# Layer B's keys and values as one Strassen product with tokens on the partitions, and the plain chunk given to the first queries

## The chip, the cores and the metric

The kernel runs on one core of a Trainium2 chip. The metric is the device time of one launch in microseconds (us), the median of three runs. The core's engines are TensorE (PE, with its weight loads as PEld), VectorE (DVE), ScalarE (ACT), GpSimd (POOL) and SyncE (SP), which here issues the DMAs. They run side by side and wait for one another by semaphores. PE writes its sums to PSUM, eight banks of 128 partitions x 512 f32; only DVE and ACT carry them from there to SBUF.

## The reference

A decoder trunk of two layers on 512 tokens of width 2048. Layer A is a sparse attention; layer B, the one in question, is a stick-breaking attention with 16 query heads over 4 shared heads of keys and values, each 128 wide. Cut to what the change touches:

```python
x = layer_norm(ALPHA * x + mixer_a(x, ...), ...)
x = x + per_layer_embed(x, p[0], ...)          # stream after layer A: 512 x 2048
k, v = jnp.split(x @ w_kv, [512], axis=-1)     # shared keys, values: 512 x 512 each
q, gate = jnp.split(x @ w_in, [2048], axis=-1) # layer B's queries and gate
o = stick_breaking(q, k, v)
h = (o * silu(gate)) @ w_o
```

All matrices are f32. `w_kv` is 2048 x 1024, its first 512 columns for the keys, the others for the values.

## The kernel before

**Numbers and products.** The stream lies transposed in SBUF: a block of 128 features by 512 tokens for each of 16 blocks (`NK`). To keep f32 precision every operand is split into a high and a low part (`split`, L140 and L141: one ACT copy to fp32r makes the high part, one DVE subtraction the low one), and each product is three matmuls (`mm3`: high x high, high x low, low x high). `XH[k]`, `XL[k]` are the parts of the stream; `F[0]` to `F[3]` hold four f32 blocks each, and `fblock(n)` is the n-th of the 16.

**Weights.** `units` lists the weight blocks in the order in which they are used. `next_raw` keeps up to three of them on the way (the tile `raw`, three buffers of 512 KB, issued by SP in order). A stream of items takes them, splits them into `wh`, `wl` and, for Strassen, `sh`, `sl` (three buffers each) and hands them to the loop that issues the matmuls. `Ahead(items, 2)` makes two items ahead of the one in use. PE's order is the program's; DVE's and ACT's is set by a scheduler, except where `paced` or `pinned` keeps the program's order.

**The stage.** At the end of layer A the stream of layer B is finished block by block. Then:

- A plain chunk (`gemm_w`, banks 0 to 3, 192 matmuls of 512 columns): the keys, four blocks of 128 columns, weights as the fixed operand, tokens moving. While it runs, `first_chunk` still splits the last blocks of the stream (`build_plain`) and makes the sums of token halves that Strassen needs (`stream_sums` into `C3`; `turn_first` writes the difference t1 over the second half of `XH[k]`, `XL[k]`).
- Five Strassen chunks (`gemm_s`, in Winograd's form, seven products in seven banks): the values, then the queries of the four groups into `F[0]` to `F[3]`. Each handles 512 output columns: the inner dimension is halved (rows k and k+8 together), the tokens are halved (256 columns per matmul) and the output blocks too. A chunk is 16 items of 21 matmuls. For each unit DVE makes four sums of weight quarters (`prepare`, s1 to s4), and each item is split in two operations on ACT and two on DVE.
- After a chunk `combine` takes the seven products together into the four quarters of the result; what it need not do at once goes into the list `bg`, whose entries `pumped_at` puts between the matmuls of the next chunk.
- In the second Strassen chunk `turn_values` transposes the values (16 transposes on PE, one ACT copy for every four), because the attention wants tokens on the partitions for them. After the fourth, `split_values` and `split_keys` write the parts that the attention uses.

The line numbers in the profile are those of this kernel; the code of DVE and ACT that goes through the wrapper `Paced` has L116 or L118, the matmuls of `mm3` have L145 to L147.

Of the kernel before, what the change touches and what calls it, by code (L numbers as in the profile page):

```python
# [18 lines left out]
T = 512  # L19
H = T // 2  # L20
D = 2048
NK = D // 128
# [55 lines left out]
def trunk_kernel(  # L78
# [17 lines left out]
    pe = nc.tensor  # L96
    pinned = [False]
# [39 lines left out]
    def bank(i, name="ps"):  # L137
        return psum.tile([128, 512], F32, name=name, tag=f"bank{i}")

    def split(hi, lo, src, eng=dve):  # L140
        act.activation(hi, src, AF.Copy)  # L141
        eng.tensor_tensor(lo, src, hi.bitcast(F32), ALU.subtract)

    def mm3(out, a, b, start, stop):
        pe.matmul(out, a[0], b[0], start=start, stop=False)  # L145
        pe.matmul(out, a[0], b[1], start=False, stop=False)  # L146
        pe.matmul(out, a[1], b[0], start=False, stop=stop)  # L147

    ident = top.tile([128, 128], F32, name="ident")
# [35 lines left out]
    halves = []  # L185
    sent = [0]

    def next_raw():
        while sent[0] < len(units) and len(raws) < 3:
            raw = top.tile([128, 2, 512], F32, name="raw", tag="raw", bufs=3)  # L190
            unit = units[sent[0]]
            if len(unit) == 1:
                _, k, n = unit[0].shape
            else:
                k, n = 2, unit[-1]
            raw = raw.rearrange("p a n -> p (a n)")[:, : k * n].rearrange("p (k n) -> p k n", k=k)
            if len(unit) == 1:
                nc.sync.dma_start(raw, unit[0])
            else:
                src, a, b, c0, n = unit  # L200
# [12 lines left out]
            raws.append(raw)  # L213
            sent[0] += 1
        return raws.popleft()
# [38 lines left out]
    def weight_parts():  # L254
        return tuple(top.tile([128, 512], F32R, name=n, tag=n, bufs=3) for n in ("wh", "wl"))
# [94 lines left out]
    def paced(fn, *args):  # L350
        was, pinned[0] = pinned[0], True
        fn(*args)
        pinned[0] = was
# [61 lines left out]
    def strassen_stream(widths, wp):  # L415
        return Ahead(strassen_items(widths, wp), 2)

    def product_banks(first):
# [25 lines left out]

    def combine(wp, M, dst):

# [20 lines left out]

    def combine_last(wp, M, dst):

# [68 lines left out]
    PAIRS = [n for k in range(8) for n in (k, k + 8)]  # L538
# [93 lines left out]
    items = Ahead(all_items(), 2)  # L632
# [85 lines left out]
    ps = bank(4, "ik")  # L718
# [15 lines left out]
    banks = late_banks(range(4))  # L734
    gemm = gemm_w(items, late_plain, banks)
# [32 lines left out]
    banks = [bank(b, "v") for b in (4, 5, 6, 7)]  # L768
# [5 lines left out]
    K = [tuple(pkv.tile([128, T], F32R, name=f"k{s}{g}") for s in "hl") for g in range(4)]  # L774
    V = [tuple(pkv.tile([128, 512], F32R, name=f"v{s}{t}") for s in "hl") for t in range(4)]
# [52 lines left out]
    for g in range(4):  # L828
        banks = [bank(b + 4 * (g % 2), "q") for b in range(4)]
# [69 lines left out]
    for g in range(4):  # L899
        banks = mm_banks("g")  # L900
# [256 lines left out]
    TF, T1, C3 = [], [], []  # L1157
# [35 lines left out]
    V, K = ([tuple(spots[n : n + 2]) for n in where] for where in ((0, 2, 4, 6), (8, 14) * 2))  # L1193
    Q, A = ([tuple(spots[n : n + 2]) for n in where] for where in ((18, 12, 16, 10), (20, 22)))

    def split_keys(g):
        split(*K[g], Kf[:, g])

    def split_values(t):
        split(*(v.rearrange("p (g d) -> p g d", g=4) for v in V[t]), Vf[:, :, t * 128 : (t + 1) * 128])  # L1200

    def split_scaled(g, i):
        qh, ql = (q.rearrange("p (h q) -> p h q", h=4) for q in Q[i])
# [3 lines left out]

    with tc.tile_pool(name="sp", bufs=1) as sp:
        Kf, Vf = shared
        banks = [bank(b, "k") for b in range(4)]  # L1210
# [5 lines left out]
        def turn_values(t):  # L1216
            s = slice(t * 128, (t + 1) * 128)
            ps = bank(2, "vt")
            for g in range(4):
                pe.transpose(ps[:, g * 128 : (g + 1) * 128], Vf[:, g, s], ident)  # L1220
            act.activation(Vf[:, :, s], ps.rearrange("p (g d) -> p g d", g=4), AF.Copy)

        for n, dst in enumerate((Vf, *F)):
            M = product_banks(4 - n)
            gemm = pumped_at(gemm_s(items, C3, M), (13, 20, 27, 34, 41, 53, 65, 77, 89, 101, 104, 107, 110))
            if n == 1:
                steps(gemm, 40)
                for t in range(4):
                    steps(gemm, 16)
                    turn_values(t)  # L1230
            run(gemm)
            drain()
            if n == 4:
# [4 lines left out]
            if n == 3:  # L1238
# [31 lines left out]
    class Sticks:  # L1270
# [3 lines left out]
        units = [(3, 3), (1, 1), (3, 2), (1, 0), (3, 1), (2, 2), (3, 0), (2, 1), (0, 0), (2, 0)]  # L1274
# [163 lines left out]
    banks = mm_banks("g")  # L1438
    items = Fed(items)
    gemm = gate_first(banks)  # L1440
# [13 lines left out]
    for g in range(4):  # L1454
# [20 lines left out]
        if g < 3:  # L1475
# [4 lines left out]
            banks = mm_banks("g")  # L1480
            gemm = gemm_w(items, plain, banks)
# [59 lines left out]
```

## Time and profile before

| | us |
|---|---|
| time, median of 3 runs | 1863.06 (1862.87 to 1863.2) |
| the profiled execution, its own time | 1863.64 |
| its span, first to last instruction | 1861.9 |
| plain chunk (keys) | 987.5 to 1031.0 |
| five Strassen chunks | 1031.0 to 1234.3 |
| transposes of the values | 1091.4 to 1110.3 |

The page gives one execution. Its busy times say how much of the span an engine worked; the chain of waits says which work, followed back from the end, set the end. A view of stretches gives, for chosen windows, the busy time and number of instructions of each engine, the clock granted to PE, the DMA engines' share and their rate. The timeline lists single instructions with start, duration, engine, line and operation, and, in brackets, how long the engine had idled and for whom. Matmuls overlap: their duration is longer than the distance to the next start.

### The profile page before, as it was taken

The page shows a single profiled execution, that of the slowest core. Times are in us where ns is not written, and L with a number is a line of the kernel's source. Part 1 is how long each engine was busy: PE and PEld are TensorE (multiplying, and loading weights), DVE is VectorE, ACT ScalarE, POOL GpSimd, SP SyncE. Part 2 cuts the span into 40 slices and gives each one's busy share as a digit, 9 for nine tenths or more (in the row PEclk, how much of TensorE's full clock was granted, in tenths as well). Part 3 has the DMA queues.
Part 4 walks back from the last instruction along what each step waited for, and adds up shares of the span by engine and source line. Part 5 has one row for each costly group of instructions (what it writes and reads, how often), then busy time and mean ns, then how long its engine had stood idle before and what let it go on. Part 6 is the DMA issues. An engine that isn't in the chain of part 4 may idle for free.

```text
span 1861.9 us, 24820 instructions
## 1 busy us (share of the span) xinstructions
PE 1854.8 (100%) x9181; PEld 1576.4 (85%) x9181; DVE 1230.9 (66%) x2395; ACT 937.7 (50%) x1688; POOL 11.8 (1%) x28
## 2 busy tenths in 40 slices
PE   9999999999999999999999999999999999999998
PEld 8898888888888888888888999988888888888887
DVE  5668678566556444676468788888878745567534
ACT  3546333355555432375245444468888733347422
POOL 0000000000000000000000000001000000000000
PEclk9999999999999999999999999999999999999999
DMA  6442333322222432332434333322122252233333
GB/s 198 128 115 68 93 100 92 101 62 71 72 60 66 159 114 85 110 111 92 140 114 129 103 103 103 103 91 91 57 69 78 69 191 92 79 125 99 116 102 114
DMA packets 111178, 189.21 MB, mean 102 GB/s; under 512 B 8528, under 2 KB 29008, under 8 KB 111056
## 3 DMA queue, kind: packets, MB, share of 16 engines
q1 hardware_dynamic: 111056, 187.62, 33.0%
q8 instruction: 72, 1.18, 0.3%
q14 instruction: 50, 0.41, 0.1%
HBM read 179.21 MB, written 8.39 MB: 101 GB/s over the span
## 4 chain that ended last, share of the span: by engine, by line
PE 97%; DVE 2%; ACT 1%; issue 0%; DMA 0%; SPq 0%
PE g L145 12%; PE g L147 12%; PE g L146 12%; PE o L147 7%; PE o L145 7%; PE o L146 7%; PE m L145 4%; PE m L147 4%; PE m L146 4%; PE q L147 3%; PE q L145 3%; PE q L146 3%; PE k L146 2%; PE k L147 2%; PE k L145 2%; PE iq L147 1%
## 5 line engine op out<-in xcount | busy, mean ns | idle before, releaser
L118 ACT ACTIVATE wh<-raw 128x512 fp32r<-128x512 f32 (+2 forms) x624 | 359.5, 577 | 685.4 <-PE g L146 219.6
L118 DVE TENSOR_TENSOR wl<-raw,wh 128x512 fp32r<-128x512 f32 (+2 forms) x623 | 387.8, 623 | 437.1 <-ACT wh L118 421.7
L145 PE MATMUL g<-xh,wh 128*128 128x512 f32 x1024 | 403.5, 394 | 0.0
L147 PE MATMUL g<-xh,wl 128*128 128x512 f32 x1024 | 399.5, 390 | 0.0
L146 PE MATMUL g<-xl,wh 128*128 128x512 f32 x1024 | 399.3, 390 | 0.0
L147 PEld LDWEIGHTS g<-xh,wl 128*128 128x128 f32 x1024 | 192.2, 188 | 41.0
L146 PEld LDWEIGHTS g<-xl,wh 128*128 128x128 f32 x1024 | 192.5, 188 | 37.2
L145 PEld LDWEIGHTS g<-xh,wh 128*128 128x128 f32 x1024 | 192.4, 188 | 36.9
L147 PE MATMUL o<-xh,wl 128*128 128x512 f32 x512 | 199.3, 389 | 0.0
L146 PE MATMUL o<-xl,wh 128*128 128x512 f32 x512 | 199.2, 389 | 0.0
L145 PE MATMUL o<-xh,wh 128*128 128x512 f32 x512 | 199.2, 389 | 0.0
L147 PEld LDWEIGHTS o<-xh,wl 128*128 128x128 f32 x512 | 96.1, 188 | 20.4 <-DVE wl L118 0.5
L146 PEld LDWEIGHTS o<-xl,wh 128*128 128x128 f32 x512 | 96.1, 188 | 20.0
L145 PEld LDWEIGHTS o<-xh,wh 128*128 128x128 f32 x512 | 96.1, 188 | 19.9
L145 PE MATMUL q<-xh,wh 128*128 128x512 f32 x256 | 99.6, 389 | 0.0
L146 PE MATMUL q<-xl,wh 128*128 128x512 f32 x256 | 99.6, 389 | 0.0
L147 PE MATMUL q<-xh,wl 128*128 128x512 f32 x256 | 99.6, 389 | 0.0
L118 ACT ACTIVATE sh<-st 128x512 fp32r<-128x512 f32 x80 | 49.7, 624 | 44.5 <-DVE st L118 44.3
L116 ACT ACTIVATE wk<-z 128x512 f32<-128x512 f32 x80 | 47.9, 598 | 38.7 <-DVE z L116 15.2
L118 DVE TENSOR_TENSOR sl<-st,sh 128x512 fp32r<-128x512 f32 x80 | 55.2, 691 | 13.9 <-ACT sh L118 13.9
L118 DVE TENSOR_TENSOR xl<-f,xh 128x512 fp32r<-128x512 f32 x80 | 54.3, 686 | 12.6 <-ACT f L118 12.3
L146 PEld LDWEIGHTS q<-xl,wh 128*128 128x128 f32 x256 | 48.0, 188 | 10.1
(298 smaller groups left out, 3401.4 us busy)
## 6 DMA issues: line engine op xcount, KB each, us to landing
raw<-w_in_a SPq DMA_DIRECT2D x95, 512.0 KB, 3.7
raw<-w_in_b SPq DMA_DIRECT2D x64, 512.0 KB, 3.8
raw<-w_ple_gate SPq DMA_DIRECT2D x52, 512.0 KB, 3.7
raw<-w_o_a SPq DMA_DIRECT2D x24, 512.0 KB, 3.8
raw<-w_o_b SPq DMA_DIRECT2D x24, 512.0 KB, 3.7
raw<-w_kv_b SPq DMA_DIRECT2D x16, 512.0 KB, 3.8
raw<-w_ple_gate SPq DMA_DIRECT2D x24, 256.0 KB, 2.9
f<-xT SPq DMA_DIRECT2D x4, 1024.0 KB, 6.4
```

What stands on the lines that cost most here:

```text
L116: ins = method(*args, **kw)
L118: ins = method(*args, **kw)
L145: pe.matmul(out, a[0], b[0], start=start, stop=False)
L146: pe.matmul(out, a[0], b[1], start=False, stop=False)
L147: pe.matmul(out, a[1], b[0], start=False, stop=stop)
```

## The change

The plain chunk and the two operands change places. The plain chunk now makes the queries of the first group into `F[0]`. The keys and values become one Strassen product of 512 tokens by 1024 columns: the stream's parts are the fixed operand (128 tokens at a time), the weights move (512 columns per matmul), and the result has tokens on the partitions. Its quarters are tokens 0 to 255 and 256 to 511 by keys and values: c11, c12 are the halves of `Kf`, c21, c22 those of `Vf`. Seven products take two banks each, so they run in three passes of 4, 4 and 6 banks, with `kv_items` reading the weights again in each pass: 8 + 8 + 16 transfers of 512 KB where there were 16. As values now come out with tokens on the partitions and keys do not come out as wanted, `turn_keys` transposes the keys in place of `turn_values` (the same number of transposes), in the query chunk for `F[2]`, and three query chunks follow in place of the values' and four.

- First pass: items are the two halves of a raw block, split and used (m2, m4). Second: the first half, and the difference s3, made by DVE (m1, m7). Third: per k, two raw blocks; POOL makes s1, DVE s2 and s4, and each of the three is split (m6, m5, m3). An item is one pair of tiles of 512 columns and feeds six matmuls. Items are made four ahead (`Ahead(kv_items(sp), 4)`), and the splits use `sh`, `sl` and `wh`, `wl` in turn.
- Up to six raw blocks are on the way in this part: every second one goes into a free half of `F[2]` or `F[3]` (`homes`).
- After the first pass ACT copies m2 and m4 out; after the second ACT copies m1 and m7, DVE adds m1 onto c11, POOL adds c22 onto c21 (1024 columns); at the end of the third ACT copies m5 and m3, DVE adds m6 onto u and m5 onto c22, and POOL does the last four sums, 1024 columns each. They replace a `combine`.
- The first query chunk's items (two) are made after 42 of the third pass's 48 steps.

In the program as built POOL's order is four of the s1 sums, the add of c22 onto c21, the other four s1 sums, then the four adds at the end. In SP's order the first transfers into `F[2]` and `F[3]` stand between the eight weight blocks of the plain chunk.

```diff
-        while sent[0] < len(units) and len(raws) < 3:
-            raw = top.tile([128, 2, 512], F32, name="raw", tag="raw", bufs=3)
+        while sent[0] < len(units) and len(raws) < (6 if sent[0] in kv_units else 3):
+            raw = homes.get(sent[0])
+            if raw is None:
+                raw = top.tile([128, 2, 512], F32, name="raw", tag="raw", bufs=3)
...
+    def kv_items(wp):
+        made = [0]
+        temps = [F[1][:, n] for n in range(4)]
+        for _ in range(2):
+            st = wp.tile([128, 4 * H], F32, name="st", tag="st", bufs=2)
+            temps.extend(st[:, n * T : (n + 1) * T] for n in range(2))
...
+        for k in range(8):
+            raw = next_raw()
+            for a in range(2):
+                yield parts(a, raw[:, a])
+        for k in range(8):
+            raw = next_raw()
+            s3 = temp()
+            dve.tensor_tensor(s3, raw[:, 0], raw[:, 1], ALU.subtract)
+            yield parts(0, raw[:, 0])
+            yield parts(1, s3)
+
+        def sums():
+            r0 = next_raw()
+            r1 = next_raw()
+            s1, s2, s4 = temp(), temp(), temp()
+            pool.tensor_tensor(s1, r0[:, 1], r1[:, 1], ALU.add)
+            dve.tensor_tensor(s2, s1, r0[:, 0], ALU.subtract)
+            dve.tensor_tensor(s4, r1[:, 0], s2, ALU.subtract)
+            return s2, s1, s4
+
+        ready = sums()
+        for k in range(8):
+            three = ready
+            for n, src in enumerate(three):
+                if n == 2 and k < 7:
+                    ready = sums()
+                yield parts(3 * k + n, src)
+
+    def gemm_quarters(items, products):
+        for k in range(NK // 2):
+            for get, outs in products:
...
+                w = next(items)
...
+                h, l = get(k)
+                for j, out in enumerate(outs):
+                    s = slice(j * 128, (j + 1) * 128)
+                    mm3(out, (h[:, s], l[:, s]), w, k == 0, k == NK // 2 - 1)
+                    yield
...
-    add_job(w_kv_b, 0, strassen=True)
-    add_job(w_kv_b, 512, strassen=True)
-    for g in range(4):
+    add_job(w_in_b, 0, strassen=True)
+    kv_rows = w_kv_b.rearrange("(k p) (a n) -> k p a n", p=128, a=2)
+    for k in (*range(8, NK), *range(8), *PAIRS):
+        kv_units.add(len(units))
+        if len(kv_units) % 2 == 0:
+            homes[len(units)] = (F[2][:, 0:2], F[2][:, 2:4], F[3][:, 0:2])[len(kv_units) // 2 % 3]
+        units.append((kv_rows[k],))
+    for g in range(1, 4):
         add_job(w_in_b, g * 512, strassen=True)
...
-        items = first_chunk(gemm, TF, T1, C3, lambda: strassen_stream([512] * 5, sp))
-        for g in range(4):
-            act.activation(Kf[:, g], banks[g], AF.Copy)
+        items = first_chunk(gemm, TF, T1, C3, lambda: Ahead(kv_items(sp), 4))
+        for h in range(4):
+            act.activation(F[0][:, h], banks[h], AF.Copy)
...
+        m2, m4 = pair(4, "m2"), pair(6, "m4")
+        run(gemm_quarters(items, ((half(8, 0), m2), (summed(2), m4))))
...
+        m1, m7 = pair(0, "m1"), pair(2, "m7")
+        run(gemm_quarters(items, ((half(0, 0), m1), (summed(1), m7))))
+        for j in range(2):
+            paced(act.activation, u[:, j], m1[j], AF.Copy)
+            paced(dve.tensor_tensor, c11[:, j], c11[:, j], m1[j], ALU.add)
+        for j in range(2):
+            paced(act.activation, c22[:, j], m7[j], AF.Copy)
+        pool.tensor_tensor(c21, c21, c22, ALU.add)
+
+        m6, m5, m3 = pair(4, "m6"), pair(6, "m5"), pair(0, "m3")
+        gemm = gemm_quarters(items, ((summed(0), m6), (half(0, H), m5), (half(8, H), m3)))
+        steps(gemm, 42)
+        pinned[0] = True
+        items = strassen_stream([512] * 3, sp).prime()
+        pinned[0] = False
...
+        pool.tensor_tensor(c21, c21, u, ALU.add)
+        pool.tensor_tensor(c22, c22, u, ALU.add)
+        pool.tensor_tensor(c12, c12, t3, ALU.add)
+        pool.tensor_tensor(c12, c12, u, ALU.add)
...
-        for n, dst in enumerate((Vf, *F)):
-            M = product_banks(4 - n)
+        for n, dst in enumerate(F[1:]):
+            M = product_banks(2 - n)
```

More of the change, by code (lines that the diff above doesn't have):

```diff
@@ L416, in strassen_stream, with temp, parts @@
         return Ahead(strassen_items(widths, wp), 2)
+    def kv_items(wp):
[4 more added lines that the diff above has]
+            temps.extend(st[:, n * T : (n + 1) * T] for n in range(2))
+        def temp():
+            made[0] += 1
+            return temps[made[0] % 8]
+        def parts(n, src):
+            if n % 2:
+                pair = weight_parts()
+            else:
+                pair = [wp.tile([128, 4, 128], F32R, name=n, tag=n, bufs=3).rearrange("p a n -> p (a n)") for n in ("sh", "sl")]
+            split(*pair, src)
+            return pair
+        for k in range(8):
[34 more added lines that the diff above has]
+                    yield
     def product_banks(first):
@@ L1209, in trunk_kernel @@
         Kf, Vf = shared
-        banks = [bank(b, "k") for b in range(4)]
+        banks = [bank(b, "q") for b in range(4)]
         gemm = gemm_w(kitems, plain, banks, order=PAIRS)
-        items = first_chunk(gemm, TF, T1, C3, lambda: strassen_stream([512] * 5, sp))
-        for g in range(4):
-            act.activation(Kf[:, g], banks[g], AF.Copy)
[L1216 to L1221, printed above, removed]
@@ L1223, in trunk_kernel, with pair, half, summed @@
-        for n, dst in enumerate((Vf, *F)):
-            M = product_banks(4 - n)
+        items = first_chunk(gemm, TF, T1, C3, lambda: Ahead(kv_items(sp), 4))
+        for h in range(4):
+            act.activation(F[0][:, h], banks[h], AF.Copy)
+        def pair(first, name):
+            return [bank(first + j, name) for j in range(2)]
+        def half(row, t):
+            return lambda k: (XH[k + row][:, t : t + H], XL[k + row][:, t : t + H])
+        def summed(i):
+            return lambda k: (C3[k][0][:, i], C3[k][1][:, i])
@@ new lines, in trunk_kernel @@
+        for j in range(2):
+            paced(act.activation, u[:, j], m1[j], AF.Copy)
+            paced(dve.tensor_tensor, c11[:, j], c11[:, j], m1[j], ALU.add)
+        for j in range(2):
+            paced(act.activation, c22[:, j], m7[j], AF.Copy)
[3 more added lines that the diff above has]
+        steps(gemm, 42)
+        pinned[0] = True
@@ new lines, in trunk_kernel @@
+        items = strassen_stream([512] * 3, sp).prime()
+        pinned[0] = False
+        steps(gemm, 2)
+        for j in range(2):
+            paced(dve.tensor_tensor, u[:, j], u[:, j], m6[j], ALU.add)
+        steps(gemm, 2)
+        for j in range(2):
+            paced(act.activation, c12[:, j], m5[j], AF.Copy)
+            paced(dve.tensor_tensor, c22[:, j], c22[:, j], m5[j], ALU.add)
+        run(gemm)
+        for j in range(2):
+            paced(act.activation, t3[:, j], m3[j], AF.Copy)
@@ new lines, in trunk_kernel, with turn_keys @@
+        pool.tensor_tensor(c21, c21, u, ALU.add)
+        pool.tensor_tensor(c22, c22, u, ALU.add)
+        pool.tensor_tensor(c12, c12, t3, ALU.add)
+        pool.tensor_tensor(c12, c12, u, ALU.add)
+        def turn_keys(g):
+            s = slice(g * 128, (g + 1) * 128)
+            ps = bank(0, "kt")
+            for t in range(4):
+                pe.transpose(ps[:, t * 128 : (t + 1) * 128], Kf[:, t, s], ident)
+            act.activation(Kf[:, :, s], ps.rearrange("p (t s) -> p t s", t=4), AF.Copy)
@@ L1227, in trunk_kernel @@
                 steps(gemm, 40)
-                for t in range(4):
+                for g in range(4):
                     steps(gemm, 16)
-                    turn_values(t)
+                    turn_keys(g)
             run(gemm)
             drain()
-            if n == 4:
+            if n == 2:
                 items = Ahead(gate_items(), 2).prime()
```

12 lines of the change are left out of this document (9 added, 3 removed).

## The prediction, made before the changed kernel was run

> **What bounds the kernel now.** I read the page's engine totals and its chain first, then the stretches of the stage that is changed, then TensorE's starts one by one.
>
> ```profile
> PE 1854.8 (100%) x9181; PEld 1576.4 (85%) x9181; DVE 1230.9 (66%) x2395; ACT 937.7 (50%) x1688; POOL 11.8 (1%) x28
> PE 97%; DVE 2%; ACT 1%; issue 0%; DMA 0%; SPq 0%
> 1030.97:1234.32 203.35, 203.35 (x1698) 203.35 (x1697) 171.09 (x353) 99.22 (x186) 0.00 (x0) 1.00 0.34 104
> ```
>
> TensorE never idles to speak of and is 97% of the chain. The third row is the five Strassen chunks (columns: stretch, length, PE, PEld, DVE, ACT and POOL busy, clock, DMA share, GB/s): PE full, DVE 84%, POOL nothing, clock 1.00. So the time moves only if PE's own work changes or if something makes PE wait. PE's price is the distance from start to start, not the duration:
>
> ```profile
> 1030.29 0.39 PE L145 MATMUL k<-xh,wh 128*128 128x512 f32 x1
> 1030.52 0.39 PE L146 MATMUL k<-xl,wh 128*128 128x512 f32 x1
> 1030.74 0.39 PE L147 MATMUL k<-xh,wl 128*128 128x512 f32 x1
> ...
> 1233.96 0.28 PE L145 MATMUL m<-c,wh 128*128 128x256 f32 x1
> 1234.08 0.28 PE L146 MATMUL m<-c,wh 128*128 128x256 f32 x1
> 1234.20 0.28 PE L147 MATMUL m<-c,wl 128*128 128x256 f32 x1
> ...
> L145 PE MATMUL k<-xh,wh x64: 389/389/389, 987.5 to 1030.3; 128*128 128x512 f32 x64
> ```
>
> A 256-column matmul starts every 0.120 us. The 192 matmuls of the plain chunk run from 987.5 to 1030.97: 0.2265 us for 512 columns. Two of 256 columns cost 0.240, so each matmul carries some 13 ns that do not shrink with it.
>
> **What PE gains.** Both kernels run one plain chunk of 192 wide matmuls (keys before, first queries after) and three Strassen query chunks. What differs is the values' chunk and one query chunk, 2 x 336 matmuls of 256 columns, against 7 products x 2 banks x 8 rows x 3 = 336 of 512. 672 x 0.120 = 80.6 us; 336 x 0.2265 = 76.1 us: **-4.5 us**. Sixteen transposes stay sixteen. That is all there is to win, and 0.24% of the time.
>
> **What feeds PE.** A pair of weight tiles ("item") now lasts six wide matmuls, 1.36 us, where a Strassen item lasted 21 x 0.120 = 2.52. Prices of feeding:
>
> ```profile
> 1080.09 0.68 DVE L118 TENSOR_TENSOR E<-E,m 128x512 f32<-128x512 f32 x1
> 1080.69 0.55 DVE L118 TENSOR_TENSOR wl<-raw,wh 128x384 fp32r<-128x384 f32 x1
> 1081.16 0.68 DVE L118 TENSOR_TENSOR sl<-st,sh 128x512 fp32r<-128x512 f32 x1
> 1081.76 0.75 DVE L118 TENSOR_TENSOR st<-raw 128x256 f32<-128x256 f32 x2
> 1082.43 0.68 DVE L118 TENSOR_TENSOR E<-E,u 128x512 f32<-128x512 f32 x1
> ...
> 1019.47 1.16 ACT L118 ACTIVATE sh<-st 128x512 fp32r<-128x512 f32 x2
> ```
>
> In a row DVE takes 0.60 per 512 columns (1080.09 to 1080.69), 0.47 per 384, 0.34 per 256; ACT 0.54 per 512 (1.16 for two, less the tail). First pass, for two items (2.72 us of PE): DVE 1.2, ACT 1.1. Second pass: DVE 1.8 with s3. Both have cover, also for the evictions between passes (ACT 4 x 0.54 = 2.2 ahead of the fifth item's split, done by about 3.4 against 4 x 1.36 = 5.44): **0**. Without the four items of lead each would cost its 2.2. The added DVE evictions (c11, u, c22: six of 0.60) replace the sixteen combine operations of the two chunks that go.
>
> Third pass, for three items (4.08 us of PE): DVE three splits and two sums, 5 x 0.60 = 3.0, and POOL one add of 512 columns, which nothing in the trace shows in that size.
>
> ```profile
> L1532 POOL MEMSET const-float32-0.0<- 128x1 f32 x1 | 0.1, 99 | 0.3 <-issue 0.3
> ...
> 1259.63 1.44 POOL L1181 TENSOR_TENSOR xl<-raw,xh 128x256 fp32r<-128x256 f32 x2 [3.99 <-DVE xh L116]
> ...
> 1276.44 1.92 POOL L1181 TENSOR_TENSOR xl<-raw,xh 128x256 fp32r<-128x256 f32 x2 [10.72 <-DVE xh L116]
> ...
> 1260.62 1.00 DVE L116 TENSOR_TENSOR wl<-raw,wh 128x512 fp32r<-128x512 f32 x1
> ...
> 1276.48 0.68 DVE L116 SCALAR_TENSOR_TENSOR wk<-z,wk 128x512 f32<-128x512 f32 x1
> 1277.08 0.68 DVE L116 TENSOR_TENSOR wl<-raw,wh 128x512 fp32r<-128x512 f32 x1
> 1277.96 0.94 DVE L116 TENSOR_TENSOR c<-wk,c 128x512 fp32r<-128x512 f32 x1 [0.20 <-ACT c L116]
> ```
>
> Undisturbed, POOL takes 0.72 for 256 columns; with 0.10 for an empty one that is 0.62 per 256, so **1.3 us for 512 and 2.6 for 1024** (between 2 and 4 times 0.62 and the same of 0.72: 1.24 to 1.44, 2.5 to 2.9). The rows also show that POOL and DVE exclude one another when both read two operands from SBUF. The DVE split at 1260.62 takes 1.00 where it takes 0.69: POOL's pair runs till 1261.07, and the split ends 0.55 later. At 1276.44 POOL's second add waits for the split at 1277.08, the pair takes 1.92 instead of 1.44, and in turn the split at 1277.96 takes 0.94. The DVE operation at 1276.48 reads z from PSUM and keeps its 0.68. The new kernel's splits and sums all read SBUF twice.
>
> The Trainium skill ("SBUF — State Buffer", section "Who interferes with whom") says that the loser blocks for the whole of the winner's instruction. The rows agree for adds of 256 columns; a 1024-column add, four times as long, no run here has yet shown. By the rule it stops DVE for all its 2.6 us; if long adds shared instead, most of the next two terms would go.
>
> *Third pass.* If they exclude one another, a round costs 3.0 + 1.3 = 4.3 against 4.08: 0.2 x 7 = 1.5 us behind. At its start ACT's c22 copies end at 2.2; then POOL's c21 add of 1024 columns holds till 4.8, and the fifth item's split, due at 5.44, ends at 5.5; two sums, the next split (1.8) and POOL's next s1 (1.3) bring the sixth to 8.6 against 6.8: 1.8 late. Together 3.3; as some of POOL's adds run while DVE waits for ACT I take **+3.0**. Bounds: 0 without exclusion; above, POOL's 8 x 1.3 + 2.6 = 13.0 less DVE's 8 x 1.08 idle, plus those 1.8: 6.
>
> *From the third pass into the next chunk.* Its third product takes m6's bank after 0.7 us, behind two DVE evictions and the primed splits: **+0.4** (0 to 1.2).
>
> *The next chunk.* Four POOL adds of 1024 columns follow at once, 10.4 us. Before, DVE was alone here:
>
> ```profile
> 1031.00:1072.00 41.00, 41.00 (x343) 41.00 (x342) 30.44 (x64) 20.10 (x38) 0.00 (x0) 1.00 0.35 107
> ```
>
> DVE is 74% busy in the first Strassen chunk, so it idles 1.3 us in a unit of two items (5.04 us). Only two items are primed; the third needs four sums and two splits (4 x 0.34 + 0.47 + 0.60 = 2.4 us), due 5.0 after the pass. If POOL gets in between each pair of DVE operations, these six stand behind all four adds: 2.4 + 10.4 = 12.8, **8 late**. If a waiting DVE is always served first, POOL enters at the first gap (DVE waits for ACT there) and each later add overruns its gap: 2.6 - 1.3, four times, less little: some 4 to 5. The rows show POOL entering at a DVE gap of 0.20 and a DVE operation going ahead between two adds; an unbroken DVE row with POOL waiting they do not show. Between 4.5 and 8 I take **+6.0**; both ends stand, and 0 without exclusion.
>
> **DMA and queues.** 32 transfers of 512 KB replace 16:
>
> ```profile
> raw<-w_kv_b SPq DMA_DIRECT2D x16, 512.0 KB, 3.8
> ...
> 10.00:20.00 10.00, 10.00 (x51) 8.99 (x50) 5.39 (x9) 4.62 (x8) 0.00 (x0) 1.00 0.74 256
> ```
>
> Pass 3 asks for two in 4.08 us, 257 GB/s; this trace moved 256 at a DMA share of 0.74. Six buffers against three give each five transfers of time, 10 us at 2.04, against 3.8 to land: 0. At 200 GB/s pass 3 would end some 3 us late. In SP's order the first three transfers into F[2] and F[3] stand among the plain chunk's eight and wait for DVE's last reads there; the raws queued behind them wait for splits of the same time, up to a lead of 10 us: 0, else one wait of a few us before pass 1. POOL's other adds (restore) come 100 us later.
>
> **Sum.** -4.5 + 3.0 + 0.4 + 6.0 = **+4.9 us** on the profiled execution's 1863.64 (span 1861.9), 1868.5; the median is 0.58 below that execution, so **1868.0**.
>
> **Rivals.**
> *The adds hide* (0.18). DVE's lead of up to three tile pairs swallows them, or long adds do not hold DVE off. Then only PE's gain and 0.4 are left: 1863.06 - 4.1 = **1859**. It decides if DVE loses under 5 us in the next chunk. For it: POOL is idle here now, and DVE has 26% spare. Against it: the stretched rows above.
> *DVE goes first nearly always* (0.12). Third pass 1.5, next chunk 3: **1863**, no change.
> *PE's clock falls in the long wait, or DMA starves pass 3* (0.10). The clock column shows 1.00 everywhere, but no inner wait this long. Half a clock for some 3 us costs 1.5 us twice, DMA 3: **1871**. The Trainium skill ("TensorE: Matmul & The Clock Gate", section "HAM oscillation — how this bites in real kernels") warns of idle gaps over about 3.4 us; no run here shows one so far.
> *The wide products do not come at 0.2265.* Every 512-column row seen has that distance whatever its operands; I give it nothing of its own.
>
> **How the numbers follow.** Forecast 0.60, with a range of its own of 1864.5 to 1873 (stalls of 6 to 14.5 less 4.5). Range for all: **1858.5 to 1873**, which leaves out half the fourth case and a tenth of the first. A change under 0.2% (3.7 us) cannot be told from none. Slower: four fifths of 0.60 and 0.10: 0.58. Same: the rest of the first and 0.12: 0.24. Faster: 0.18.
>
> **What would show it.** Wide products 0.2265 apart and the stage 4.5 us shorter where PE does not wait: the gain. Waits of PE on the "wl" and "sl" tiles about the sixth item of the third pass, and 4 to 8 us at the third item of the next chunk, with DVE rows there of 2 us and more beside POOL's adds: the losses. POOL adds of 1024 columns well under 2 us, DVE rows at 0.69 beside them, or PE without waits after the passes would make it wrong; waits on DMA would show the fourth case.

## The result, and the profile after

| | before | after |
|---|---|---|
| time, median of 9 runs each, us | 1863.06 (1862.73 to 1863.45) | 1867.88 (1867.2 to 1868.66) |
| ratio after to before | | 1.0026 (95% interval 1.0016 to 1.0037) |
| the profiled execution, its own time, us | 1863.64 | 1868.31 |
| its span, us | 1861.9 | 1866.6 |
| the stage: end of the plain chunk to the first matmul of the attention, us | 203.35 | 209.13 |

The change costs 4.8 us. The page of after, engine totals and chain:

```profile
PE 1852.5 (99%) x8845; PEld 1561.0 (84%) x8845; DVE 1233.7 (66%) x2337; ACT 940.0 (50%) x1686; POOL 36.7 (2%) x41
PE 96%; DVE 2%; issue 1%; ACT 1%; DMA 0%; SPq 0%; DVEq 0%; ACTq 0%
```

PE has 336 matmuls fewer and is no longer at 100% of a longer span. POOL's busy time has grown by 25 us. DMA and SP's queue stand at 0% of the chain, though twice as much of `w_kv_b` is read.

The stage in two stretches, the wide products and the three query chunks (columns: stretch, length, PE, PEld, DVE, ACT and POOL busy, clock, DMA share, GB/s), and PE's starts around its two waits:

```profile
1029.91:1107.62 77.71, 76.61 (x337) 62.91 (x336) 64.07 (x88) 39.76 (x69) 14.97 (x9) 1.00 0.57 190
1107.62:1239.04 131.42, 125.55 (x1026) 125.32 (x1025) 111.96 (x215) 61.44 (x116) 9.90 (x4) 0.97 0.33 97
```

```profile
1080.23 0.39 PE L145 MATMUL m<-wh,xh 128*128 128x512 f32 x1
...
1081.72 0.50 PE L146 MATMUL m<-wl,xh 128*128 128x512 f32 x1 [1.10 <-DVE wl L118]
...
1112.83 0.28 PE L146 MATMUL m<-xl,wh 128*128 128x256 f32 x1
1118.98 0.58 PE L147 MATMUL m<-xh,wl 128*128 128x256 f32 x1 [5.88 <-DVE wl L118]
...
1124.70 0.30 PE L146 MATMUL m<-c,sh 128*128 128x256 f32 x1
```

PE waits twice for DVE. The third pass begins 192 wide matmuls after 1029.91, at 1073.4; the first wait, at 1080.23, is 6.8 us later: the sixth item (five of 1.36 us are used up). It costs 1081.72 - 1080.23 - 0.23 = 1.26 us. Ahead of it the timeline of after shows POOL's add of c22 onto c21 (L1314) and a sum s1 (L458) one behind the other, and DVE gets one operation through for each:

```profile
1076.58 2.85 POOL L1314 TENSOR_TENSOR E<-E 128x1024 f32<-128x1024 f32 x1
1077.20 2.77 DVE L118 TENSOR_TENSOR f<-f,f 128x512 f32<-128x512 f32 x1
1079.39 1.73 POOL L458 TENSOR_TENSOR st<-raw,f 128x512 f32<-128x512 f32 x1
1079.90 1.76 DVE L118 TENSOR_TENSOR wl<-st,wh 128x512 fp32r<-128x512 f32 x1
```

The last of these rows is the split for which PE waits. The second wait is in the third item of the next chunk: 1118.98 - 1112.83 - 0.12 = 6.03 us. Then 26 matmuls take from 1118.98 to 1124.70, 5.72 us, where 26 x 0.120 = 3.12 was their price before: 2.6 us more, with nothing to wait for. The clock column says why, in steps of 2 us of after:

```profile
1114.00:1116.00 2.00, 0.00 (x0) 0.00 (x0) 1.98 (x1) 0.00 (x0) 2.00 (x2) 1.00 0.00 0
1116.00:1118.00 2.00, 0.00 (x0) 0.00 (x0) 1.99 (x1) 0.00 (x0) 2.00 (x1) 0.98 0.00 0
1118.00:1120.00 2.00, 1.02 (x4) 1.02 (x5) 1.77 (x4) 1.51 (x4) 0.18 (x1) 0.50 0.00 0
...
1122.00:1124.00 2.00, 2.00 (x11) 2.00 (x11) 1.70 (x4) 1.34 (x3) 0.00 (x0) 0.50 0.62 214
1124.00:1126.00 2.00, 2.00 (x16) 2.00 (x15) 2.00 (x5) 0.33 (x1) 0.00 (x0) 0.82 0.26 40
```

PE does nothing from 1114 to 1118, while DVE and POOL are both "busy" all the time; near 1118 the granted clock drops to 0.50, so PE's first 5.7 us of work after the wait run at the lower clock, a matmul every 0.22 us on average instead of 0.120. What DVE and POOL were busy with, from the timeline of after:

```profile
1108.05 1.28 DVE L118 TENSOR_TENSOR E<-E,m 128x512 f32<-128x512 f32 x2
1108.28 2.41 POOL L1332 TENSOR_TENSOR E<-E,f 128x1024 f32<-128x1024 f32 x1 [13.85 <-DVE f L118]
1109.24 4.26 DVE L118 TENSOR_TENSOR st<-raw 128x256 f32<-128x256 f32 x2
1110.64 2.58 POOL L1334 TENSOR_TENSOR E<-E,f 128x1024 f32<-128x1024 f32 x1
1113.18 2.52 POOL L1333 TENSOR_TENSOR E<-E,f 128x1024 f32<-128x1024 f32 x1
1113.42 2.56 DVE L118 TENSOR_TENSOR st<-st,raw 128x256 f32<-128x256 f32 x1
1115.66 2.52 POOL L1335 TENSOR_TENSOR E<-E,f 128x1024 f32<-128x1024 f32 x1
1116.01 2.44 DVE L118 TENSOR_TENSOR st<-raw,st 128x256 f32<-128x256 f32 x1
1118.38 0.55 DVE L118 TENSOR_TENSOR wl<-raw,wh 128x384 fp32r<-128x384 f32 x1
```

These rows are turn-taking. DVE's sums of 256 columns, 0.34 us from one to the next in the trace of before, last 2.44 and 2.56 us (4.26 for a pair): one of them ends each time one of POOL's adds has ended. The eviction at 1108.05, which reads `m` from PSUM, keeps its 1.28 us for two while POOL's first add runs. POOL's adds start 2.36 us apart beside that eviction and 2.54 and 2.48 apart beside DVE's sums, so a sum takes at most 0.2 us from POOL. PE's wait ends 0.80 us after the fourth add (1115.66 + 2.52 = 1118.18): the last sum, then the split of 0.55.

### The profile page after: what moved, and what is told of

It is laid out like the page before. It is cut to its first block, busy times and chain, and to the rows that moved or that the text cites. A ratio compares the mean times of both kernels' runs of the same rounds, so it can differ in the third digit from the quotient of the medians.

```text
span 1866.6 us, 24141 instructions
## 1 busy us (share of the span) xinstructions
PE 1852.5 (99%) x8845; PEld 1561.0 (84%) x8845; DVE 1233.7 (66%) x2337; ACT 940.0 (50%) x1686; POOL 36.7 (2%) x41
## 4 chain that ended last, share of the span: by engine, by line
PE 96%; DVE 2%; issue 1%; ACT 1%; DMA 0%; SPq 0%; DVEq 0%; ACTq 0%
PE g L145 12%; PE g L147 12%; PE g L146 12%; PE o L146 7%; PE o L145 7%; PE o L147 7%; PE q L147 4%; PE q L146 4%; PE q L145 4%; PE m L147 3%; PE m L146 3%; PE m L145 3%; PE iq L147 1%; PE iq L146 1%; PE iq L145 1%; PE pt L949 1%
## 5 line engine op out<-in xcount | busy, mean ns | idle before, releaser
L118 ACT ACTIVATE wh<-raw 128x512 fp32r<-128x512 f32 (+2 forms) x596 | 345.3, 580 | 660.7 <-PE g L146 219.6
L118 DVE TENSOR_TENSOR wl<-raw,wh 128x512 fp32r<-128x512 f32 (+2 forms) x595 | 372.9, 628 | 432.3 <-ACT wh L118 417.3
L145 PE MATMUL q<-xh,wh 128*128 128x512 f32 x320 | 124.5, 389 | 0.0
L146 PE MATMUL q<-xl,wh 128*128 128x512 f32 x320 | 124.5, 389 | 0.0
L147 PE MATMUL q<-xh,wl 128*128 128x512 f32 x320 | 124.5, 389 | 0.0
L146 PEld LDWEIGHTS q<-xl,wh 128*128 128x128 f32 x320 | 60.1, 188 | 12.6
L145 PEld LDWEIGHTS q<-xh,wh 128*128 128x128 f32 x320 | 60.1, 188 | 12.6
L147 PEld LDWEIGHTS q<-xh,wl 128*128 128x128 f32 x320 | 60.1, 188 | 12.3
```

The costliest lines, as they stand in the source:

```text
L118: ins = method(*args, **kw)
```

## The experiments

In all of them the stage is measured like above, from the start of the first product after the plain chunk to the first `z` matmul, and split where the 256-column matmuls begin. The median of before lay between 1863.08 and 1863.27 us in the sets of runs beside them.

### The four closing sums on DVE

```diff
-        pool.tensor_tensor(c21, c21, u, ALU.add)
-        pool.tensor_tensor(c22, c22, u, ALU.add)
-        pool.tensor_tensor(c12, c12, t3, ALU.add)
-        pool.tensor_tensor(c12, c12, u, ALU.add)
+        for c, s in ((c21, u), (c22, u), (c12, t3), (c12, u)):
+            bg.extend(lambda c=c[:, j], s=s[:, j]: dve.tensor_tensor(c, c, s, ALU.add) for j in range(2))
```

> The changed kernel with the four 1024-column POOL adds behind the third pass made by DVE, as eight adds of 512 columns spread over the next chunk (the pieces of the list bg). Theory (POOL and DVE take turns at reading SBUF, an add of 2.5 us for every DVE operation): the wait of 6.0 us at the third item of that chunk goes, and with it the half clock behind it (some 2.7 us); the added DVE work, 8 x 0.60 in 40 us with 26% idle, is hidden: 1867.9 - 8.7 = 1859.2 (1858.6 to 1860.5), clock 1.00. Rival (the item is late because DVE has too much to do there, whoever adds): DVE has 4.8 us more to do, so no better than 1867.

Measured: 1860.55 us (1859.88 to 1861.04), ratio 0.9985 (0.9975 to 0.9994). The two stretches, and all that PE waited for in them:

```profile
1030.44:1108.17 77.73, 76.62 (x337) 62.91 (x336) 64.32 (x88) 39.83 (x69) 15.84 (x9) 1.00 0.60 190
1108.17:1230.95 122.78, 122.78 (x1025) 122.76 (x1024) 108.33 (x223) 61.48 (x116) 0.00 (x0) 1.00 0.35 104
```

```profile
PE m L146 <- DVE wl L118: 1.1, 1, 1.1
```

The query chunks take 122.78 instead of 131.42 us: the whole wait and the whole spell at half clock are gone, 8.64 us, with the same additions done by DVE. The rival falls. The median is 0.05 above the range given: the stage is 8.62 us shorter than that of after (209.13 - 200.51), but the medians differ by 7.33. In the two profiled executions 0.53 us of that lies ahead of the stage, which began at 1029.91 in after and at 1030.44 here, and 0.37 behind the last matmul ("Still open" below). The wide products keep their 77.7 us.

### The same sums on POOL, in pieces of 256 columns

```diff
-        pool.tensor_tensor(c21, c21, u, ALU.add)
-        pool.tensor_tensor(c22, c22, u, ALU.add)
-        pool.tensor_tensor(c12, c12, t3, ALU.add)
-        pool.tensor_tensor(c12, c12, u, ALU.add)
+        for c, s in ((c21, u), (c22, u), (c12, t3), (c12, u)):
+            for j in range(2):
+                for t in (slice(0, H), slice(H, T)):
+                    pool.tensor_tensor(c[:, j, t], c[:, j, t], s[:, j, t], ALU.add)
```

> The changed kernel with the same four sums left on POOL, but cut into sixteen adds of 256 columns. Theory of turns: POOL is busy as long as before (16 x 0.62 = 10 us), but each of the six DVE operations of the third item waits for one add of 0.6 us only: ready about 1 us late instead of 6, no fall of the clock: 1867.9 - 5 - 2.7, about 1860.5 (1859.5 to 1862). Rival (POOL's total time counts, DVE is held off until POOL is done): the wait stays, 1868.

Measured: 1865.6 us (1864.61 to 1866.46), ratio 1.0013 (1.0004 to 1.0022), between the two and a miss. The timeline of this kernel:

```profile
1107.95 14.46 POOL L1335 TENSOR_TENSOR E<-E,f 128x256 f32<-128x256 f32 x16 [12.65 <-DVE f L118]
...
1111.17 0.95 DVE L118 TENSOR_TENSOR st<-st,raw 128x256 f32<-128x256 f32 x1
1112.16 0.84 DVE L118 TENSOR_TENSOR st<-raw,st 128x256 f32<-128x256 f32 x1
1112.92 1.09 DVE L118 TENSOR_TENSOR wl<-raw,wh 128x384 fp32r<-128x384 f32 x1
1113.94 1.23 DVE L118 TENSOR_TENSOR sl<-st,sh 128x512 fp32r<-128x512 f32 x1
```

```profile
1119.51 0.28 PE L146 MATMUL m<-xl,wh 128*128 128x256 f32 x1
1121.87 0.38 PE L147 MATMUL m<-xh,wl 128*128 128x256 f32 x1 [2.07 <-DVE wl L118]
```

The turns are still one for one: a DVE operation becomes 0.4 to 0.55 us longer (a sum's row lasts 0.84 to 0.95 instead of 0.42, a split's 1.09 instead of 0.55 and 1.23 instead of 0.69), not a whole long add. So the third item is only 0.85 and 0.34 us late, as the theory had it. But there are now sixteen turns. They take 14.46 us where 10 had been expected, so POOL loses by them too (0.90 us a piece instead of 0.62); they last to 1122.4, and the fifth item is late as well, by 2.24 us. That was not foreseen. The clock was 0.67 in the stretch from 1122 to 1124 and 0.50 in the next: after a wait of 2.24 us. Cutting the adds up moves the loss; it does not remove it.

### The kernel before, with four such adds and nothing else

Four POOL additions of 1024 columns, whose result nothing uses, start with the first Strassen chunk of the old kernel.

```diff
         for g in range(4):
             act.activation(Kf[:, g], banks[g], AF.Copy)
+        for _ in range(4):
+            pool.tensor_tensor(F[3][:, 0:2], Kf[:, 2:4], F[3][:, 2:4], ALU.add)
```

> The kernel before, with four POOL adds of 1024 columns more (keys plus a dead block of F[3], written to dead space) where its first Strassen chunk begins. Theory: there the sums of the third item are made already, so only its two splits and the next item's two stand behind the four adds, one each: two waits of PE of some 2 and 2.5 us, each under 3.4 us, so the clock stays: 1863.1 + 4.5 = 1867.5 (1866 to 1869). Rival (the loss belongs to the new layout, not to POOL's adds): 1863.1.

Measured: 1867.74 us (1866.88 to 1868.47), ratio 1.0024 (1.0015 to 1.0034), stage 208.44 us, +5.09. The timeline, DVE and POOL first, then PE, then a stretch:

```profile
1031.52 10.52 POOL L1216 TENSOR_TENSOR f<-E,f 128x1024 f32<-128x1024 f32 x4 [842.85 <-ACT E L118]
1031.88 2.47 DVE L118 TENSOR_TENSOR wl<-raw,wh 128x384 fp32r<-128x384 f32 x1 [1.07 <-ACT wh L118]
1034.27 2.89 DVE L118 TENSOR_TENSOR sl<-st,sh 128x512 fp32r<-128x512 f32 x1
```

```profile
1040.58 0.28 PE L146 MATMUL m<-c,sh 128*128 128x256 f32 x1
1042.65 0.39 PE L147 MATMUL m<-c,sl 128*128 128x256 f32 x1 [1.79 <-DVE sl L118]
```

```profile
1044.00:1046.00 2.00, 2.00 (x11) 2.00 (x11) 1.77 (x5) 1.91 (x4) 0.00 (x0) 0.50 0.01 4
```

Four adds alone make the old kernel 4.5 us slower, so neither the new layout nor the extra weight traffic is needed for such a loss. That it is near the 4.8 us of the whole change is chance: in the changed kernel four such adds cost 8.64. The time lies in the range by luck. Two waits of 4.5 us in all had been expected and a clock that stays up; PE waited 0.58, 0.77 and 1.95 us within some 6 us, 3.30 in all, and the clock still fell, from 1043.4 to 1046.8, for the other 1.8. In the ten runs of this kernel the times stand in two groups of five, 1866.88 to 1867.26 and 1868.21 to 1868.47, 1.2 us apart. The mean clock recorded with each run is 0.999 in all of the upper group and 1.000 in four of the lower five, which would fit a spell that is missing there; that stays a guess, as only an execution of the upper group was profiled.

### The kernel before, with POOL writing instead of adding

Ten memsets of 1024 columns, with a result that nothing uses, in the same place.

```diff
+        pool.tensor_copy(F[3][:, 0, 0:1], Kf[:, 3, 0:1])
+        for _ in range(10):
+            pool.memset(F[3][:, 0:2], 0.0)
```

> The kernel before, with ten POOL memsets of 1024 columns into the same dead space at the same place, in place of the adds: POOL is as busy (about 10 us), but reads nothing from SBUF (but for one column, so that it starts there). Theory that reading is what excludes: no change, 1863.1. Rival (any work of POOL on SBUF holds DVE off): two waits as with the adds, about 1867.

Measured: 1863.77 us (1863.3 to 1863.92), ratio 1.0002 (0.9993 to 1.0011), which cannot be told from no change; stage 203.36 us against 203.35 before.

```profile
1031.48 10.05 POOL L1217 MEMSET f<- 128x1024 f32 x10
...
1032.13 0.69 DVE L118 TENSOR_TENSOR sl<-st,sh 128x512 fp32r<-128x512 f32 x1
```

POOL is busy as long as with the four adds, and the split beside it keeps 0.69 us. So it is not POOL being at work that excludes, nor its writing, but its reading beside a DVE operation that reads two operands; a POOL operation with one operand was not tried.

### The add of c22 onto c21 taken off POOL

This and the next start from the version with the closing sums on DVE.

```diff
-        pool.tensor_tensor(c21, c21, c22, ALU.add)
...
         pinned[0] = False
+        for j in range(2):
+            paced(dve.tensor_tensor, c21[:, j], c21[:, j], c22[:, j], ALU.add)
```

> As adds_on_dve, and the add of c22 onto c21 too is taken from POOL: DVE makes it, 2 x 512 columns, after the third pass's last splits. POOL keeps only its eight s1 sums. Theory: the wait of 1.3 us at the sixth item of the third pass came from that add (2.85 us in which DVE could start one operation only), so it goes and the two short ones with it: the stage from the first wide product to the attention falls from 200.5 to about 198.9 us, the time from 1860.55 to 1859.0 (1858.6 to 1859.6). Rival (the s1 sums alone put DVE behind, 4.3 us of turns against 4.08 in each round, or the four evictions on ACT do): a wait of 1 us and more stays, 1860.3.

The second leaves this as it is and moves the eight sums s1 to DVE as well:

```diff
-            pool.tensor_tensor(s1, r0[:, 1], r1[:, 1], ALU.add)
+            dve.tensor_tensor(s1, r0[:, 1], r1[:, 1], ALU.add)
```

> As c21_late, with the eight s1 sums on DVE too, so that POOL does nothing in the product. Theory: nobody takes turns any more, but DVE has 6 x 0.60 = 3.6 us in a round of 4.08 instead of 3.0 beside 1.3 of POOL's: no wait either, 1859.0 (1858.6 to 1859.8). If c21_late still waits and this does not, the s1 sums were the cause; if both wait alike, it is DVE's own work or ACT's evictions. Rival (DVE is too full without POOL's help): waits of 1 to 3 us, 1860 to 1862.

Measured: 1860.34 us (1860.12 to 1860.65) and 1859.75 us (1859.57 to 1859.99), ratios 0.9985 and 0.9982 (intervals up to 0.9994 and 0.9991). The first is a miss by 0.7 us. The second lies within its range, but by luck: its stage is as long as the first's (200.12 and 200.13 us), and PE waits in its query chunks too, though no wait had been forecast. The stretches of c21_late:

```profile
1030.45:1106.61 76.16, 76.16 (x338) 63.06 (x336) 62.07 (x88) 39.76 (x69) 12.28 (x8) 1.00 0.61 194
1106.61:1230.58 123.97, 123.58 (x1026) 122.92 (x1025) 109.54 (x225) 61.38 (x116) 0.00 (x0) 1.00 0.35 102
```

The wide products now take 76.16 us, 336 x 0.2267: no wait is left in the third pass, so its 1.55 us go when that one add of 1024 columns goes, and the eight sums s1 alone on POOL cost PE nothing there. But the query chunks are 1.2 us longer. Why, in the timeline of the same kernel:

```profile
1105.84 1.29 DVE L118 TENSOR_TENSOR E<-E 128x512 f32<-128x512 f32 x2
...
1107.04 1.28 DVE L118 TENSOR_TENSOR f<-f,m 128x512 f32<-128x512 f32 x2
...
1107.87 0.36 PE L145 MATMUL m<-c,sh 128*128 128x256 f32 x1 [0.39 <-ACT wh L118]
```

The moved addition (1105.84) stands ahead of the evictions of m6 and m5 (the first at 1107.04), whose banks the next chunk's products need. PE's wait is put down to ACT's `wh`, which is not what was late; the eviction of m6's first bank ends in the middle of it. The place where POOL's add cost 1.55 us was traded for one where DVE's cost 1.2.

### All the sums behind the evictions

The list `bg` of the next chunk gets the addition too, as its first two entries. In these two kernels m5 is already in c22 when c22 is added, so c21 takes in m5 as well; the instructions are of the same number and size.

```diff
-        for j in range(2):
-            paced(dve.tensor_tensor, c21[:, j], c21[:, j], c22[:, j], ALU.add)
...
-        for c, s in ((c21, u), (c22, u), (c12, t3), (c12, u)):
+        for c, s in ((c21, c22), (c21, u), (c22, u), (c12, t3), (c12, u)):
```

> Kernel after with the add of c22 onto c21 and the four closing sums as ten DVE additions of 512 columns, all of them put among the next chunk's steps, behind the evictions of m6, m5 and m3; POOL keeps only the eight sums s1. Theory (a POOL add beside the splits makes DVE late, and so does a DVE addition that stands ahead of an eviction; an addition behind the evictions costs nothing): both halves of the stage are free of waits, 76.1 us for the 336 wide matmuls as in c21_late and 122.8 us to the attention as in adds_on_dve, 198.9 us in all against 203.35 before, so 1863.1 - 4.45 = 1858.6 us (1858.2 to 1859.4). Rival (ten additions are more than DVE's spare time in the next chunk holds): a wait at that chunk's third or fifth item and, where it is over 2 us, half the clock behind it, so 1861 us or more.

> As sums_all_late, with the eight sums s1 on DVE too, so that POOL does none of the stage's sums. Theory (eight s1 additions cost the third pass nothing on either engine, since c21_late and no_pool spent the same 76.16 us there): stage 198.9 us, 1858.6 us (1858.2 to 1859.4), the same as sums_all_late within 0.5 us. Rival (DVE, with the s1 sums and ten more, falls behind its items): the stage is 1 us or more longer than that of sums_all_late.

Measured: 1859.16 us (1858.88 to 1859.78) and 1858.68 us (1858.29 to 1858.95); stages 198.94 us (76.16 + 122.78) and 198.92. PE waits for nothing in either: this is the change without its losses, 4.41 us shorter than before.

### Two versions that make the whole product

In the first, ACT alone copies m5 out, and DVE adds that copy onto c22 in `bg`: twelve additions there; once with POOL's s1, once without.

```diff
-            paced(dve.tensor_tensor, c22[:, j], c22[:, j], m5[j], ALU.add)
...
-        for c, s in ((c21, c22), (c21, u), (c22, u), (c12, t3), (c12, u)):
+        for c, s in ((c21, c22), (c22, c12), (c21, u), (c22, u), (c12, t3), (c12, u)):
```

> As sums_all_late, but only ACT copies m5 out, into c12, and DVE adds that copy onto c22 among the next chunk's steps, behind the add of c22 onto c21: twelve DVE additions there, which together with POOL's s1 make the whole of the product. Theory (additions that stand behind the evictions are free): stage 198.9 us as in sums_all_late, 1859 us (1858.3 to 1859.7), faster than both kernels. Rival (twelve are too many, or the copy of m5 by ACT alone frees its banks later): the next chunk is 0.5 us or more longer than the 122.8 us of sums_all_late.

> As m5_by_act, with the eight s1 sums on DVE, so that POOL does none of the stage's sums. Theory: stage 198.9 us, 1858.8 us (1858.2 to 1859.5), the same as m5_by_act within 0.5 us. Rival (POOL's s1 sums do cost something that the stage does not show, as the medians of c21_late and no_pool, 0.6 us apart, would have it): m5_by_act is slower by 0.4 us or more though the stage is the same length.

Measured: 1859.8 us (1859.47 to 1860.25) and 1859.26 us (1858.88 to 1859.62); the first 0.1 above its range, the second inside it. But both stages, 199.62 and 199.63 us, are 0.7 us over the forecast: the rival's price. The timeline of m5_by_act, DVE, then PE:

```profile
1146.97 0.68 DVE L118 TENSOR_TENSOR E<-E,f 128x512 f32<-128x512 f32 x1
1147.58 0.68 DVE L118 TENSOR_TENSOR f<-m,u 128x512 f32<-128x512 f32 x1
```

```profile
1147.97 0.28 PE L147 MATMUL m<-xh,wl 128*128 128x256 f32 x1
1148.32 0.39 PE L145 MATMUL m<-c,sh 128*128 128x256 f32 x1
```

The twelfth addition (1146.97) now stands ahead of the chunk's own evictions (`f<-m,u`), and the chunk after it waits for a bank. Ten entries fitted, twelve did not.

In the second, DVE adds m7 from its banks straight onto c21 behind the second pass, in the place where it adds m1; eight additions remain in `bg`, and the sums s1 are on DVE.

```diff
         for j in range(2):
             paced(act.activation, c22[:, j], m7[j], AF.Copy)
+            paced(dve.tensor_tensor, c21[:, j], c21[:, j], m7[j], ALU.add)
...
-        for c, s in ((c21, c22), (c21, u), (c22, u), (c12, t3), (c12, u)):
+        for c, s in ((c21, u), (c22, u), (c12, t3), (c12, u)):
```

> As no_pool, but DVE adds m7 from its banks straight onto c21 behind the second pass (two additions of 512 columns, at the place where it adds m1 onto c11), so c21 += c22 is gone from the start of the next chunk and eight additions stand behind the evictions there, as in adds_on_dve. The whole product is made. Theory (the 1.28 us of DVE time at the start of the third pass fits its spare time, and nothing else is late): stage 198.9 us as in no_pool_late, 1858.7 us (1858.2 to 1859.3), the fastest of the kernels that make the whole product. Rival (DVE has no 1.28 us to spare there, where POOL's add of 2.85 us made PE wait 1.6): the third pass takes 0.5 us or more over 76.16 us, 1859.3 us or more.

Measured: 1858.66 us (1858.42 to 1859.2), ratio 0.9976 (0.9966 to 0.9985), the fastest that makes the whole product. Its stage:

```profile
1030.93:1229.87 198.94, 198.94 (x1362) 185.82 (x1361) 169.41 (x320) 100.75 (x184) 0.00 (x0) 1.00 0.45 138
```

PE is busy for all of the 198.94 us, as it was for the 203.35 of before. DVE does every sum that POOL had and is busy for 169.41 us, less than beside POOL (176.03 us in after), since part of that was waiting counted as work.

## Why the prediction was right, and where only in sum

The median was forecast at 1868.0 us and came to 1867.88. The terms, against the stage of the profiled execution (+5.78 us):

| term | forecast | measured |
|---|---|---|
| PE's gain | -4.5 | -4.41 (203.35 - 198.94) |
| third pass | +3.0 (0 to 6) | +1.55 (77.71 - 76.16) |
| into the next chunk | +0.4 (0 to 1.2) | 0 |
| next chunk, the wait | +6.0 (0, 4.5 to 8) | +6.03 |
| next chunk, the clock | rival, 0.10 | +2.61 (131.42 - 122.78 - 6.03) |
| sum | +4.9 | +5.78 |

*PE's gain* was right: 512 columns come every 0.227 us in this place too, and a stage without waits is 4.41 us shorter.

*The third pass* was mis-sized. Its second part was right in place and nearly in size: POOL's add onto c21 makes the sixth item late, by 1.26 us where 1.8 was worked out, and 0.29 follow in steps of 0.1 and less. Its first part, 0.2 us lost in each round, is there in DVE's rows but not as a wait of PE. In c21_late, where the eight s1 adds are alone on POOL, the third pass reads:

```profile
1082.84 1.46 POOL L458 TENSOR_TENSOR f<-raw,f 128x512 f32<-128x512 f32 x1 [2.77 <-DMA f<-w_kv_b]
1083.07 1.78 DVE L118 TENSOR_TENSOR wl<-f,wh 128x512 fp32r<-128x512 f32 x1
...
1087.29 1.78 DVE L118 TENSOR_TENSOR sl<-st,sh 128x512 fp32r<-128x512 f32 x1
```

A split lasts 1.78 instead of 0.69, as the add had begun before it, and the five operations of this round take 4.22 us against PE's 4.08. Four rounds lose 0.15 us each in this way, not seven, since half of the s1 sums are made before the sixth item. DVE's lead, from the end of an item's split to the matmul that reads it, shrinks by that from 2.1 us at the sixth item to 1.5 at the eighteenth. The forecast charged the loss to PE at once; it left out the lead that swallows it.

*Into the next chunk* PE lost no more than 0.1 us; the evictions of m6 came in time.

*The next chunk's wait* was right in place (third item), releaser (`wl` of DVE) and size, but the size lay between two ways of taking turns and only one of them happened: POOL gets in between each pair of DVE operations, the upper end, worked out as 12.8 - 5.0 = 7.8. Two parts of that were too much. The sums' own 4 x 0.34 us were added to POOL's 10.4, and three of the four pass beside the adds; and `sl`, 0.60 us, comes behind `wl`, for which PE waits. So 0.80 us followed the last add instead of 2.4. The rest nearly cancels: the adds began 0.66 us after the pass but took 9.90 instead of 10.4, and PE needed that `wl` 5.33 us after the pass instead of 5.0. 7.8 - 1.6 - 0.2 = 6.0. The middle had been taken for not knowing which way it goes, so its exactness is luck.

*The clock* is where the forecast left out a real term. It was given 0.10 and a time of 1871, as a case that takes the place of the forecast. It was rather a consequence of the forecast: a wait of 6 us is just what makes the clock fall, and it should have been in the same sum. The Trainium skill ("TensorE: Matmul & The Clock Gate", section "HAM oscillation — how this bites in real kernels") warns of idle gaps over about 3.4 us; the 6.03 us of after agree. The 2.24 us of adds_in_256 and the three waits of old_plus_adds, none over 1.95 us, do not: here less was enough.

*That the median was right all the same* is cancelling. In the stage 2.6 us of clock were missing, against 1.85 us too much for the third pass and the transition: with 0.1 of PE's gain the sum is 0.9 us short. In the profiled executions the stage began 1.06 us earlier in after than in before. The kernels made from after leave the parts ahead of the stage as they are, and there it begins between 1030.13 and 1030.93, so most of this is how executions differ. The medians are 4.82 us apart.

*The rivals.* "The adds hide" is refuted by after itself, and the rule that it was weighed against holds for long adds too: by the Trainium skill ("SBUF — State Buffer", section "Who interferes with whom") the loser blocks for the whole instruction, and a sum of 0.34 us lasted 2.44 beside a 1024-column add of 2.52. "DVE goes first nearly always" is refuted by the same rows. DMA and the queues were rightly put at 0: no wait of PE in the stage is for a transfer, though 231 GB/s were moved over 22 us of it in after:

```profile
1053.00:1075.00 22.00, 22.00 (x98) 18.21 (x97) 19.63 (x28) 12.31 (x21) 4.10 (x3) 1.00 0.70 231
```

*Still open.* With only the sums s1 on POOL the median is higher than with none by 0.59 (c21_late, no_pool), 0.48 (sums_all_late, no_pool_late) and 0.54 us (m5_by_act, m5_by_act_no_pool). The stage is equally long in each pair to 0.02 us, and so, to 0.1, is the way from it to the last matmul. The difference lies at the very end: from the start of the last matmul to the end of the span it is 5.7 us in the three with s1 on POOL (1858.5 - 1852.79 in m5_by_act) and 5.2 to 5.3 in the three without (1857.3 - 1852.03), with the same instructions in the records there. All of it is in POOL's last steps, behind all other work: its last DRAIN ends 0.49 us later (5.52 us after that start in c21_late and m5_by_act, 5.53 in sums_all_late, 5.03 to 5.04 without s1 on POOL). But it ends at 5.05 in after too, which has s1 and five more adds on POOL. Why POOL's end takes this half microsecond longer was not found.

## What to carry to other kernels

An idle engine is not free help: before a step goes to POOL, see whether DVE reads two SBUF operands at the same time and how much lead the consumer has; each long add can then cost DVE its whole length, and DVE, busy for 74% of the first Strassen chunk of before, did the same sums for nothing once they stood where nobody waited for it. A moved operation must also not stand ahead of an eviction: the same 1.28 us of additions cost 1.2 us before the evictions of m6 and m5, 0 behind them, and 0.7 when two entries too many ran into the next chunk's. When a forecast contains a wait of PE of some microseconds, add the spell at half clock that follows it to the same case.

## What the hardware showed that was not expected

POOL and DVE take strict turns, one instruction each, when both have work that excludes the other: four adds let four DVE operations through, and beside sixteen short adds every DVE operation that reads SBUF twice is 0.4 to 0.55 us longer. A memset on POOL, or an eviction on DVE that reads one operand from PSUM, goes on beside the other engine at its own speed (0.69 and 1.28 us).

The granted clock fell after PE had been idle for 6.03 us, for 2.24, and for 3.3 in three waits within some 6 us, and not after 1.26 us alone. It stayed at 0.50 for 6.8, 3.4 and 3.4 us (1117.9 to 1124.7 in after; 1122.7 to 1126.1 in adds_in_256; 1043.4 to 1046.8 in old_plus_adds), even though PE worked without a pause in the last of them. Counted back from each fall in steps of 3.41 us, PE was busy for 0, 1.34 and 1.62 us in the step that ends at the fall, and for 2.02, 3.41 and 2.38 us in the step before, after which the clock stayed at 1.00. From 0.50 it rose after steps with 3.42, 3.27 and 3.41 us of work and not after the one with 2.34 (after, from 1117.91). This would fit a clock that is set anew every 3.41 us or so by how much PE worked in the step just past; it rests on three falls and was not tried by itself.
